# A two-layer streaming encoder on one core: the mixer's element-wise work moved to VectorE, its chains re-spaced, PSUM as one pool of eight banks, and the second half's column sums issued later

## The chip, the core and the metric

The kernel runs on one core of a Trainium2 chip. The engines are PE (TensorE: matrix products, and transposes through the identity), VectorE (DVE), ScalarE (ACT), GpSimd (POOL) and SyncE (SP, which issues the DMAs). PE writes into PSUM, which has eight banks of 512 fp32 columns; VectorE and ScalarE read the banks. The metric is the device time of one execution in microseconds, as the median of several runs.

## What is computed

Two groups of requests share all weights: 512 rows of a new stream and 64 rows of a running one, 576 rows in all, of width 1024. In each of two layers:

```
x = x + 0.5 * post1(SwiGLU_1(pre1(x)))                  # FFN 1, inner width 2816
z = pre2(x) @ w_in                                      # one projection, 2240 columns
mix = concat[MLA(512) | HGRN2(256) | chunk-gMLP(256)] @ w_out
x = x + post2(mix)
x = x + 0.5 * post3(SwiGLU_2(pre3(x)))                  # FFN 2
```

pre and post are RMS norms. The three mixers are:

```
MLA:    c = rmsnorm(kv_a); k_pe = rope(kpe)             # latent, also an output
        p = softmax(q_lat c^T + q_pe k_pe^T), by chunks of 64
        o = (p c) w_uv                                  # 4 heads
HGRN2:  b = cumsum(log f) in a chunk of 64
        S' = exp(b_last) S + sum_s k exp(b_last - b_s) v_s^T
        o  = (q exp(b)) S + (q k^T with decay exp(b_t - b_s), causal) v
        o  = rmsnorm(o, out_g) * silu(g)                # 4 heads of 64
gMLP:   v = rmsnorm(gelu(cv)) ; out = gelu(cu) * (tril(w_s) v + b_s)
```

## The kernel before

Activations stand transposed, the 1024 channels as eight tiles of 128 partitions, the 576 rows as columns, in two **halves** of 288. Each fp32 product is made of three matmuls on a high and a low part (wh and wl of a weight, hh and hl of an activation: L126/L127 split the weights, `split` at L138 to L142 the activations). FFN units (tile u) and projections (tile n) are such triples.

A stage starts with the norm of its input, half by half. `pre` (L185) splits a tile and adds its squares into acc; `pre_stats` then waits, asks PE for the column sums of acc (tile ss, at `colsum`), makes 1/rms (m at L209, the power on GpSimd at L151, tile rn) and, 3.11 us of virtual time later, has PE spread it over the partitions (tile bc). An FFN's units need only hh and hl, and their evacuation needs rbc, the copy of bc. Where the next stage's units are issued among the end of this one, the code calls it packed: mixer to FFN 2 and FFN 2 to layer 1.

In the mixer, five tiles of rows go through w_in. HGRN2's sum over a chunk is cut into seven **levels** h (with two key tiles m each, 14 in all, generator `make(n)` at L700 ff.): two subtractions make differences of b (L707, L708, tile e), ScalarE takes their exponential (L709), GpSimd multiplies by k (L711, tile w), VectorE by q (L717, tile zb, two operations of 64 partitions), PE forms the products lv and ls, and VectorE copies them under a mask into at and ats (L732, L739). Gelu and Silu of the projections (L888, L892) are activations of the tables other than Exp; a change of function between two activations costs a table load. Then state products (su, L819/L821), output norms (`out`, L845/L847, `group_norm` with its power on GpSimd at L151), the gMLP (`cmlp`, L862/L863), latents (`latent`, cn at L908, flipped by PE into cth and ctl), the cache chain (`caches`, ck, kp, cch, ccl), the rotary key, the queries and the attention.

What sets the order: the program is written by one main line that issues the dense products, and a list of background generators. `mul` and `flip` add each product's estimated time to a clock self.t; `tick` resumes a generator once its due time has come, and a `yield 8.0` is a wait of 8 us of that virtual clock. Every engine then runs its instructions in the order in which they were written, except for moves by the scheduler, which keeps that order as a priority; `pin` (keep_in_program_order) forbids such a move. Tiles come from pools: a new tile takes the buffer of an older one and waits until that one's last reader is done. PSUM has the pool mm (six banks) for products and sm (two) for flips, sums and spreads.

## Time and profile before

| | before |
|---|---|
| median of 3 runs | 2283.32 us (2280.43 to 2283.41) |
| profiled execution: its time, its span | 2281.2 us, 2279.4 us |
| mean granted clock of PE | 0.985 |
| PE busy | 2209.0 us, 97% |
| VectorE, ScalarE, GpSimd busy | 1552.8, 1093.7, 157.1 us |

The profile is one execution. Busy time is shown by engine, and the granted clock is a share of 2.4 GHz, with 1.2 GHz as the lower level, so that a window's mean between 0.5 and 1 tells how much of it ran at either. Matmuls are pipelined: one lasts longer than the distance to the next start. "Idle before" an instruction is put down to what released it last. FFN 1 of layer 0 ends at about 440 us, mixer 0 runs from there to about 740, and FFN 2 follows. The transitions named in the prediction are mixer to FFN 2 (at 741 and 1862 us) and FFN 2 to layer 1 (1145 us).

### The profile page before, as it was taken

The numbers are of one execution on the slowest core, as the hardware profiler recorded it, in microseconds if no ns is written. First come the engines' busy times: TensorE is split into PE (matmuls) and PEld (weight loads), VectorE is DVE, ScalarE is ACT, GpSimd is POOL, SyncE is SP. The second block draws the span as 40 slices with busy tenths as digits, with TensorE's granted clock in tenths as the row PEclk, the third lists the DMA queues.
The fourth block names the chain that finished last, engine by engine and source line by source line (L and its number), as shares of the span: only waits on it lengthen the run. The fifth ranks groups of instructions, "written<-read, shape, count | busy, mean of one in ns | idle before, by whom it ended". The sixth has DMA issues, their size and how long they took to land.

```text
span 2279.4 us, 39545 instructions
## 1 busy us (share of the span) xinstructions
PE 2209.0 (97%) x15988; PEld 2152.9 (94%) x15988; DVE 1552.8 (68%) x2697; ACT 1093.7 (48%) x1917; POOL 157.1 (7%) x160
## 2 busy tenths in 40 slices
PE   8999999998899899999999999999988999999998
PEld 8999999988799899999989999998887999999998
DVE  5888643787566888844488875438976578887443
ACT  7454442465554544443354444325746545444423
POOL 0000000143300000000000000001432000000000
PEclk9999999999999999999999999999999999999999
DMA  7333442312212233344223334423121222333421
GB/s 218 91 96 93 121 134 84 105 46 78 62 53 83 90 91 102 87 127 130 61 80 102 93 94 126 128 75 102 40 88 48 75 98 79 94 93 102 121 70 42
DMA packets 339531, 211.07 MB, mean 93 GB/s; under 512 B 17378, under 2 KB 319700, under 8 KB 339348
## 3 DMA queue, kind: packets, MB, share of 16 engines
q1 hardware_dynamic: 339348, 208.54, 30.6%
q8 instruction: 126, 2.06, 0.4%
q14 instruction: 57, 0.47, 0.1%
HBM read 190.11 MB, written 18.38 MB: 91 GB/s over the span
## 4 chain that ended last, share of the span: by engine, by line
PE 83%; DVE 9%; ACT 3%; issue 2%; POOL 2%; DMA 0%; SPq 0%; POOLq 0%; DVEq 0%; ACTq 0%
PE d L68 25%; PE X L68 20%; PE Q L68 10%; PE u L68 9%; PE R L68 5%; PE wo L68 5%; PE n L68 2%; DVE zb L717 1%; PE sc L68 1%; DVE wl L127 1%; PE q L68 1%; DVE hl L142 1%; PE oT L68 1%; POOL gr L151 1%; DVE acc L198 1%
## 5 line engine op out<-in xcount | busy, mean ns | idle before, releaser
L68 PE MATMUL d<-gh,wh 128*128 128x288 f32 x1408 | 414.0, 297 | 2.7 <-ACT gh L138 2.7
L68 PE MATMUL d<-gl,wh 128*128 128x288 f32 x1408 | 414.6, 295 | 0.0
L68 PE MATMUL d<-gh,wl 128*128 128x288 f32 x1408 | 413.5, 295 | 0.0
L127 DVE TENSOR_TENSOR wl<-wr,wh 128x1024 fp32r<-128x1024 f32 (+3 forms) x190 | 222.4, 1176 | 168.4 <-ACT wh L126 167.3
L126 ACT ACTIVATE wh<-wr 128x1024 fp32r<-128x1024 f32 (+3 forms) x190 | 191.6, 1012 | 276.8 <-PE d L68 167.4
L68 PEld LDWEIGHTS d<-gh,wh 128*128 128x128 f32 x1408 | 262.7, 188 | 3.6 <-ACT gh L138 3.6
L68 PEld LDWEIGHTS d<-gh,wl 128*128 128x128 f32 x1408 | 265.2, 189 | 0.0
L68 PEld LDWEIGHTS d<-gl,wh 128*128 128x128 f32 x1408 | 264.3, 188 | 0.0
L68 PE MATMUL X<-th,wh 128*128 128x288 f32 x864 | 256.1, 296 | 0.0
L68 PE MATMUL X<-tl,wh 128*128 128x288 f32 x864 | 255.4, 296 | 0.0
L68 PE MATMUL X<-th,wl 128*128 128x288 f32 x864 | 254.5, 295 | 0.0
L68 PE MATMUL u<-hl,wh 128*128 128x288 f32 x736 | 221.2, 302 | 2.2 <-DVE hl L142 2.0
L68 PE MATMUL u<-hh,wh 128*128 128x288 f32 x736 | 217.3, 305 | 3.0 <-ACT x L1377 1.5
L68 PE MATMUL u<-hh,wl 128*128 128x288 f32 x736 | 219.6, 301 | 0.0
L138 ACT ACTIVATE wh<-wr 128x1024 fp32r<-128x1024 f32 x144 | 151.6, 1056 | 136.1 <-PE R L68 68.5
L139 DVE TENSOR_TENSOR wl<-ws,wh 128x1024 fp32r<-128x1024 f32 x108 | 132.3, 1225 | 102.1 <-ACT wh L138 102.1
L138 ACT ACTIVATE wh<-ws 128x1024 fp32r<-128x1024 f32 x108 | 114.6, 1061 | 148.1 <-DVE ws L508 100.1
L139 DVE TENSOR_TENSOR wl<-wr,wh 128x1024 fp32r<-128x1024 f32 x144 | 175.3, 1220 | 7.4 <-ACT wh L138 6.2
L398 DVE TENSOR_TENSOR d<-d,d 128x288 f32<-128x288 f32 x128 | 55.3, 454 | 181.9 <-PE d L68 181.7
L68 PEld LDWEIGHTS X<-th,wl 128*128 128x128 f32 x864 | 163.1, 189 | 0.0
L68 PEld LDWEIGHTS X<-tl,wh 128*128 128x128 f32 x864 | 162.3, 188 | 0.0
L68 PEld LDWEIGHTS X<-th,wh 128*128 128x128 f32 x864 | 162.1, 188 | 0.0
(364 smaller groups left out, 5562.5 us busy)
## 6 DMA issues: line engine op xcount, KB each, us to landing
wr<-ffn_w_gate SPq DMA_DIRECT2D x144, 256.0 KB, 3.0
wr<-ffn_w_up SPq DMA_DIRECT2D x144, 256.0 KB, 3.4
wr<-ffn_w_down SPq DMA_DIRECT2D x64, 512.0 KB, 4.3
wr<-w_in SPq DMA_DIRECT2D x30, 512.0 KB, 3.7
xd<-x SPq DMA_DIRECT2D x48, 288.0 KB, 2.1
x<-xd SPq DMA_DIRECT2D x48, 288.0 KB, 5.8
wr<-ffn_w_down SPq DMA_DIRECT2D x32, 384.0 KB, 3.6
wr<-ffn_w_gate SPq DMA_DIRECT2D x16, 512.0 KB, 3.7
```

Source lines behind the costliest of these rows:

```text
L68: self.nc.tensor.matmul(out, lhsT, rhs, start=start, stop=stop, skip_group_check=onto)
L126: nc.scalar.activation(hi[:, :a * b], raw[:, :a * b], AF.Copy)
L127: nc.vector.tensor_tensor(lo[:, :a * b], raw[:, :a * b], hi[:, :a * b].bitcast(F32), op=ALU.subtract)
L138: nc.scalar.activation(hi, src, AF.Copy)
L139: nc.vector.tensor_tensor(lo, src, hi.bitcast(F32), op=ALU.subtract)
L142: nc.vector.scalar_tensor_tensor(lo, src, scale, hi.bitcast(F32), op0=ALU.mult, op1=ALU.subtract)
L151: self.nc.gpsimd.tensor_tensor(out, m, self.mhalf[:, :n], op=ALU.pow)
L198: nc.vector.tensor_tensor(self.acc[:, sl], self.acc[:, sl], sq[:, sl], op=ALU.add)
L398: nc.vector.tensor_tensor(d[m][:, sl], d[m][:, sl], ps[hf][:, :n], op=ALU.add)
L717: nc.vector.tensor_tensor(zo, qv[rs, :, h:], ev[rs, :, h:], op=ALU.mult)
```

## The change

- `sm` becomes `mm`: one PSUM pool of eight banks in place of six and two.
- `pre_stats` of the second half waits 14.0 in place of 5.0 where stages are packed, 7.0 elsewhere.
- HGRN2: q times k (L692), the level product and e times k go from GpSimd to VectorE. The level product covers only the first half of each block and is made in place in e. Exp, Gelu and Silu are pinned. The pace of the levels is 2.2 for 3.0.
- Group norm and gate (`out`, `cmlp`) are one operation for each group of 64 columns; hgrn_out_g becomes a scale in the split of the mixed rows (four rows more in the table `more`).
- Query sums (accq) go from GpSimd to VectorE, the PSUM copies of v (L1172) from ScalarE to VectorE.
- The yields of caches, latents, rotary key, query norm, state loop, outputs and gMLP are longer, and the cache and rotary chains are spawned ahead of the query units.

```diff
@@ -56,7 +56,7 @@
         self.t = 0.0
-        self.pace, self.apace, self.l1, self.l2, self.l3 = 3.0, 2.16, 1.26, 3.94, 2.15
+        self.pace, self.apace, self.l1, self.l2, self.l3 = 2.2, 2.16, 1.26, 3.94, 2.15
@@ -109,10 +109,10 @@
     def mm(self, s="mm"):
-        return self.ps.tile([P, 512], F32, name=self.name(s), tag="mm", bufs=6)
+        return self.ps.tile([P, 512], F32, name=self.name(s), tag="mm", bufs=8)
     def sm(self, s="sm"):
-        return self.ps.tile([P, 512], F32, name=self.name(s), tag="sm", bufs=2)
+        return self.mm(s)
@@ -260,7 +260,7 @@
                 yield (1.25, 1.3)[half]
-        yield from self.pre_stats(half, (3.97, 5.0)[half])
+        yield from self.pre_stats(half, 3.97 if half == 0 else 14.0 if self.packed else 7.0)
@@ -569,7 +569,7 @@
             nc.sync.dma_start(kpv[:, :, e], i["cache_mla_kpe"][l, 0].rearrange("(t p) d -> p t d", p=P))
-        yield 8.0
+        yield 14.0
@@ -637,15 +637,15 @@
         self.rsqrt(r, ss, 4)
-        return r.unsqueeze(2).to_broadcast([P, 4, 64])
-
-    def to_mix(self, src, k0, i):
+        return r
+
+    def to_mix(self, src, k0, i, scale=(None, None)):
         for e in range(2):
-            self.split(self.mixh[k0 + e][:, c:c + w], self.mixl[k0 + e][:, c:c + w], ps[:, e * P:e * P + w])
+            self.split(self.mixh[k0 + e][:, c:c + w], self.mixl[k0 + e][:, c:c + w], ps[:, e * P:e * P + w], scale=scale[e])
@@ -692,7 +692,7 @@
             qk.append(self.slot("qk"))
-            nc.gpsimd.tensor_tensor(qk[m], q[m], kk[m], op=ALU.mult)
+            nc.vector.tensor_tensor(qk[m], q[m], kk[m], op=ALU.mult)
@@ -706,16 +706,16 @@
             nc.vector.tensor_tensor(ev[:, :, h:], bv[:, :, h:], rb, op=ALU.subtract)
-            nc.scalar.activation(e[:, c0:], e[:, c0:], AF.Exp)
-            w = self.slot("w")
-            nc.gpsimd.tensor_tensor(w[:, c0:], kk[m][:, c0:], e[:, c0:], op=ALU.mult)
+            self.pin(nc.scalar.activation(e[:, c0:], e[:, c0:], AF.Exp))
                 nc.vector.tensor_tensor(zo, qv[rs, :, h:], ev[rs, :, h:], op=ALU.mult)
-            ready[n] = (w, z)
+            kv = kk[m][:, c0:].rearrange("p (b x) -> p b x", x=2 * h)
+            nc.vector.tensor_tensor(ev[:, :, :h], ev[:, :, :h], kv[:, :, :h], op=ALU.mult)
+            ready[n] = (e, z)
@@ -782,10 +782,10 @@
                                     bv[:, :, P - 1:P].to_broadcast([P, 4, P]), bv, op=ALU.subtract)
-            nc.scalar.activation(e, e, AF.Exp)
+            self.pin(nc.scalar.activation(e, e, AF.Exp))
             eb[m] = self.slot("eb")
-            nc.scalar.activation(eb[m], b[m], AF.Exp)
-            nc.gpsimd.tensor_tensor(e, e, kk[m], op=ALU.mult)
+            self.pin(nc.scalar.activation(eb[m], b[m], AF.Exp))
+            nc.vector.tensor_tensor(e, e, kk[m], op=ALU.mult)
@@ -822,7 +822,7 @@
                         nc.sync.dma_start(dst, new[s, s])
-                yield 0.1
+                yield 1.2
@@ -842,28 +842,29 @@
             on = self.slot("on")
-            nc.vector.tensor_tensor(on[:, :256].rearrange("p (g d) -> p g d", g=4),
-                                    ps[:, :256].rearrange("p (g d) -> p g d", g=4), r, op=ALU.mult)
-            nc.vector.tensor_tensor(on[:, :256], on[:, :256], vg[i][:, 256:512], op=ALU.mult)
-            yield 7.71
-            self.to_mix(on, 4, i)
+            for g in range(4):
+                gs = slice(g * 64, (g + 1) * 64)
+                nc.vector.scalar_tensor_tensor(on[:, gs], ps[:, gs], r[:, g:g + 1], vg[i][:, 256 + g * 64:320 + g * 64],
+                                               op0=ALU.mult, op1=ALU.mult)
+            yield 9.0
+            self.to_mix(on, 4, i, [self.og[:, 2 * l + e:2 * l + e + 1] for e in range(2)])
             self.spawn(out(i))
-            yield 1.12
+            yield 3.2
         r = self.group_norm(v)
-        vv = v.rearrange("p (g d) -> p g d", g=4)
-        nc.vector.tensor_tensor(vv, vv, r, op=ALU.mult)
-        nc.gpsimd.tensor_tensor(v, v, c["vg"], op=ALU.mult)
+        for g in range(4):
+            gs = slice(g * 64, (g + 1) * 64)
+            nc.vector.scalar_tensor_tensor(v[:, gs], v[:, gs], r[:, g:g + 1], c["vg"][:, gs], op0=ALU.mult, op1=ALU.mult)
             nc.sync.dma_start(self.o["cmlp_v"][l, 0], v[:64])
-        yield 4.28
+        yield 8.0
@@ -875,7 +876,7 @@
                                            op0=ALU.add, op1=ALU.mult)
-        yield 6.56
+        yield 8.0
@@ -885,12 +886,11 @@
         for i in range(5):
-            nc.scalar.activation(uv[i][:, :512], uv[i][:, :512], AF.Gelu_apprx_tanh)
-            self.spawn(self.cmlp(l, i, uv[i], c), 0.8 + 2.59 * i)
+            self.pin(nc.scalar.activation(uv[i][:, :512], uv[i][:, :512], AF.Gelu_apprx_tanh))
+            self.spawn(self.cmlp(l, i, uv[i], c), 1.5 + 5.0 * i)
             g = vg[i][:, 256:512]
-            nc.scalar.activation(g, g, AF.Silu)
-            nc.gpsimd.tensor_tensor(g, g, c["og"], op=ALU.mult)
+            self.pin(nc.scalar.activation(g, g, AF.Silu))
@@ -910,7 +910,7 @@
             nc.sync.dma_start(self.o["ckv_p"][l, 0, (i - 1) * P:i * P], cn[:, :256])
-        yield 4.0
+        yield 8.0
@@ -942,7 +942,7 @@
         kpt = a["kpt"] = self.slot("kpth", F32R), self.slot("kptl", F32R)
-        yield 4.0
+        yield 10.0
@@ -950,12 +950,12 @@
                 self.split(kpt[0][:, cs], kpt[1][:, cs], tp[:, e * P:e * P + twid(i)])
-            yield 0.32
+            yield 2.0
         a["sq"] = self.small("sqs", 6, 2)
-        yield 1.34
+        yield 5.0
@@ -1065,7 +1065,6 @@
-        c["og"] = self.gain_rows("hgrn_out_g", l)
@@ -1099,6 +1098,8 @@
             self.step(self.bg[-1])
+        lat.append(self.spawn(self.rotary_key(l, kr, a), 9.0))
+        cg = self.spawn(self.caches(l, c), 0.0)
@@ -1114,9 +1115,7 @@
                     nc.scalar.activation(sq[:, sl], p[:, :n], AF.Square)
-                    nc.gpsimd.tensor_tensor(accq[:, sl], accq[:, sl], sq[:, sl], op=ALU.add)
-        cg = self.spawn(self.caches(l, c), 0.0)
-        lat.append(self.spawn(self.rotary_key(l, kr, a), 1.0))
+                    nc.vector.tensor_tensor(accq[:, sl], accq[:, sl], sq[:, sl], op=ALU.add)
@@ -1169,7 +1168,7 @@
                 self.mul(ps, xl, uw[0][:, ct], False, ct == 1)
-            nc.scalar.activation(t[:, :512], ps, AF.Copy)
+            nc.vector.tensor_copy(t[:, :512], ps)
@@ -1294,8 +1293,8 @@
         ps = self.sm("tp")
-        self.flip(ps[:, :18], more)
-        nc.vector.tensor_copy(self.colg[:, 96:], ps[:, :18])
+        self.flip(ps[:, :22], more)
+        nc.vector.tensor_copy(self.colg[:, 96:], ps[:, :22])
@@ -1326,7 +1325,7 @@
-        pin = tc.keep_in_program_order
+        pin = self.pin = tc.keep_in_program_order
@@ -1353,7 +1352,7 @@
             self.mul(self.warm[:, :P], self.ones, self.ones, True, True)
-        self.colg = const.tile([P, 114], F32, name="colg", tag="colg")
+        self.colg = const.tile([P, 118], F32, name="colg", tag="colg")
@@ -1384,11 +1383,13 @@
         self.ahead += [self.cols(*q) for q in todo[2:4]]
-        more = const.tile([18, P], F32, name="more", tag="more")
+        more = const.tile([22, P], F32, name="more", tag="more")
         nc.sync.dma_start(more[10:18], i["cmlp_b_s"].rearrange("l g t -> (l g) t"))
+        nc.sync.dma_start(more[18:22], i["hgrn_out_g"].rearrange("l (k p) -> (l k) p", p=P))
         self.bs = self.colg[:, 106:114]
+        self.og = self.colg[:, 114:118]
         self.spawn(self.pre_stats(1, 7.5, sums))
```

The first place is PE at the entry of FFN 2 in layer 0. bc is the spread of the first half, ss the column sums of the second, u_8281 and u_8282 are units of the first half, u_8361 and on those of the second. Before:

```order
L68 MATMUL u_8282<-hl_8137,wh_8088 128x288
L68 MATMUL u_8282<-hh_8136,wl_8089 128x288
L73 MATMUL bc_8309<-ident_c,rn_7922 128x64
L73 MATMUL bc_8309<-ident_c,rn_7922 128x128 x2
L68 MATMUL ss_8401<-ones,acc_7920 128x1 x3
L68 MATMUL u_8361<-hh_8164,wh_7796 128x288
L68 MATMUL u_8361<-hl_8165,wh_7796 128x288
L68 MATMUL u_8361<-hh_8164,wl_7797 128x288
```

After:

```order
L68 MATMUL u_8461<-hh_8164,wl_8083 128x288
L68 MATMUL u_8462<-hh_8164,wh_8088 128x288
L68 MATMUL u_8462<-hl_8165,wh_8088 128x288
L68 MATMUL u_8462<-hh_8164,wl_8089 128x288
L68 MATMUL ss_8475<-ones,acc_7920 128x1 x3
L68 MATMUL u_8461<-hh_8207,wh_8082 128x288
L68 MATMUL u_8461<-hl_8208,wh_8082 128x288
L68 MATMUL u_8461<-hh_8207,wl_8083 128x288
```

ss now stands 108 rows behind the first u_8361 (u_8461 and u_8462 are the last of these 108), where it stood just ahead of it.

The second place is PE at the entry of mixer 0: ss are the column sums of the first half and bc its spread, u_4818 and u_4819 before (u_4819 and u_4820 after) units whose half follows. Before:

```order
L68 MATMUL u_4611<-hh_4688,wl_4358 128x288
L68 MATMUL ss_4764<-ones,acc_4454 128x1 x3
L68 MATMUL u_4612<-hl_4689,wh_4363 128x288
L68 MATMUL u_4612<-hh_4688,wl_4364 128x288
L68 MATMUL u_4818<-hh_4502,wl_4346 128x288
...
L68 MATMUL u_4818<-hh_4594,wh_4345 128x288
L73 MATMUL bc_4809<-ident_c,rn_4456 128x64
L73 MATMUL bc_4809<-ident_c,rn_4456 128x128 x2
```

After:

```order
L68 MATMUL u_4613<-hl_4690,wh_4364 128x288
L68 MATMUL ss_4765<-ones,acc_4455 128x1 x3
L68 MATMUL u_4613<-hh_4689,wl_4365 128x288
L73 MATMUL bc_4810<-ident_c,rn_4457 128x64
L73 MATMUL bc_4810<-ident_c,rn_4457 128x128 x2
L68 MATMUL u_4819<-hh_4503,wh_4346 128x288
L68 MATMUL u_4819<-hl_4504,wh_4346 128x288
```

Between ss and bc stood 25 matmuls, and one is left; the others follow bc.

The third place is VectorE among the levels, where e_5189 (before) and e_5208 (after) are the differences of one level. Before:

```order
L127 TENSOR_TENSOR wl_5555<-wr_5552,wh_5554 128x960
L732 COPY_PREDICATED at_5090<-lmask_c,lv_5212 128x8x32
L732 COPY_PREDICATED at_5092<-lmask_c,lv_5212 128x8x32
L739 COPY_PREDICATED ats_5063<-lmask_c,ls_5219 64x2x32
L717 TENSOR_TENSOR zb_5007<-z_4608,e_5189 64x288 x2
L707 TENSOR_TENSOR e_5222<-b_5025 128x18x16
L708 TENSOR_TENSOR e_5222<-b_5025 128x18x16
L127 TENSOR_TENSOR wl_5561<-wr_5558,wh_5560 128x960
```

After:

```order
L732 COPY_PREDICATED at_5090<-lmask_c,lv_5198 128x8x32
L739 COPY_PREDICATED ats_5061<-lmask_c,ls_5205 64x2x32
L708 TENSOR_TENSOR e_5208<-b_5024 128x18x16
L127 TENSOR_TENSOR wl_5249<-wr_5246,wh_5248 128x1024
L715 TENSOR_TENSOR zb_5008<-z_4608,e_5208 64x288 x2
L717 TENSOR_TENSOR e_5208<-e_5208,k_5012 128x18x16
L732 COPY_PREDICATED at_5119<-lmask_c,lv_5258 128x8x32
L732 COPY_PREDICATED at_5121<-lmask_c,lv_5258 128x8x32
L739 COPY_PREDICATED ats_5061<-lmask_c,ls_5265 64x2x32
```

The multiplication of e by k, which was GpSimd's, stands behind the zb pair; the lines moved by two (zb is L715 now, the new product L717).

## Rows read from the trace of the kernel before

**Rows 1.** The page, part 1: busy time of each engine, share of the span, instructions.
```profile
PE 2209.0 (97%) x15988; PEld 2152.9 (94%) x15988; DVE 1552.8 (68%) x2697; ACT 1093.7 (48%) x1917; POOL 157.1 (7%) x160
```

**Rows 2.** Windows: each engine's busy us (instructions), granted PE clock, DMA share, GB/s.
```profile
520.00:540.00 20.00, 16.14 (x99) 15.19 (x98) 17.00 (x33) 11.89 (x20) 5.76 (x5) 0.84 0.33 103
600.00:620.00 20.00, 15.86 (x80) 13.40 (x80) 8.79 (x28) 13.84 (x33) 3.21 (x3) 0.83 0.11 30
620.00:640.00 20.00, 18.12 (x123) 17.36 (x122) 12.06 (x29) 11.31 (x27) 0.98 (x1) 0.91 0.09 27
627.00:684.00 57.00, 57.00 (x430) 55.05 (x429) 34.21 (x103) 31.62 (x83) 0.00 (x0) 0.98 0.19 54
741.00:764.00 23.00, 17.06 (x111) 16.51 (x110) 20.90 (x49) 13.97 (x31) 2.72 (x2) 0.85 0.35 126
1145.00:1170.00 25.00, 19.53 (x133) 18.98 (x132) 22.55 (x56) 13.77 (x33) 2.68 (x3) 0.86 0.35 123
1862.00:1890.00 28.00, 22.05 (x147) 21.51 (x147) 25.04 (x59) 15.38 (x34) 3.71 (x3) 0.82 0.35 123
```

**Rows 3.** Timeline of PE in mixer 0: start us, duration us, operation, tiles.
```profile
531.49 0.31 PE L68 MATMUL n<-wh,hl 128*128 128x320 f32 x1
...
536.41 0.47 PE L68 MATMUL n<-wl,hh 128*128 128x320 f32 x1
```

**Rows 4.** Waits of PE from 440 to 660 us: total us, times, longest us.
```profile
PE tp L73 <- DVE cn L908: 3.9, 1, 3.9
PE v L68 <- ACT cch L138: 2.2, 1, 2.2
...
PE lv L68 <- DVE zb L717: 1.0, 1, 1.0
...
PE tp L73 <- ACT kd L803: 0.3, 1, 0.3
```

**Rows 5.** Waits of PE over the whole span.
```profile
PE ss L68 <- DVE acc L198: 16.3, 3, 5.4
```

**Rows 6.** Timeline of PE at the entry of FFN 2, layer 0; [idle before it and its releaser].
```profile
756.94 1.44 PE L68 MATMUL ss<-ones,acc 128*128 128x1 f32 x6 [5.42 <-DVE acc L198]
```

**Rows 7.** Timeline of PE and VectorE at the entry of mixer 0.
```profile
431.45 0.72 PE L68 MATMUL ss<-ones,acc 128*128 128x1 f32 x6
...
435.41 0.16 DVE L209 TENSOR_SCALAR m<-ss 128x3 f32<-128x3 f32 x1
...
436.55 0.63 PE L73 MATMUL bc<-ident_c,rn 64*128 64x64 f32 x3 [0.44 <-POOL rn L151]
```

**Rows 8.** Timeline of VectorE in the levels of mixer 0.
```profile
500.01 0.77 DVE L732 COPY_PREDICATED at<-lmask_c,lv 128x256 f32<-128x256 int32 x2
...
500.81 0.44 DVE L707 TENSOR_TENSOR e<-b 128x288 f32<-128x288 f32 x1
501.18 0.44 DVE L708 TENSOR_TENSOR e<-b 128x288 f32<-128x288 f32 x1
502.37 2.07 DVE L717 TENSOR_TENSOR zb<-z,e 64x288 f32<-64x288 f32 x2 [0.75 <-ACT e L709]
```

**Rows 9.** Timeline of GpSimd beside the last of these.
```profile
502.42 1.71 POOL L711 TENSOR_TENSOR w<-k,e 128x576 f32<-128x576 f32 x1 [2.75 <-PE ls L68]
```

**Rows 10.** Line 717 over the span: ns min/median/max, first and last start.
```profile
L717 DVE TENSOR_TENSOR zb<-z,e x56: 416/480/1687, 467.9 to 1658.0; 64x288 f32<-64x288 f32 x48, 64x256 f32<-64x256 f32 x8
```

**Rows 11.** Groups of PE from 440 to 540 us: busy us, mean ns | idle before.
```profile
L68 PE MATMUL lv<-zb,w 128*128 128x128 f32 x104 | 13.8, 276 | 1.0 <-DVE zb L717 1.0
```

**Rows 12.** Timeline of ScalarE in the levels.
```profile
504.23 0.63 ACT L888 ACTIVATE uv<-uv 128x512 f32<-128x512 f32 x1
504.88 1.28 ACT L709 ACT_TABLE_LOAD   x1
506.17 0.68 ACT L709 ACTIVATE e<-e 128x576 f32<-128x576 f32 x1
```

**Rows 13.** Groups of VectorE from 440 to 640 us.
```profile
L139 DVE TENSOR_TENSOR ccl<-tp,cch 128x512 fp32r<-128x512 f32 x1 | 0.7, 691 | 2.6 <-ACT cch L138 2.6
```

## The prediction

> **What bounds the kernel now.** The engine row of the page comes first: PE is busy 97% of the span, VectorE 68%, ScalarE 48%, GpSimd 7% [rows 1]. A change can only gain where PE idles or where its clock is down, so I next read PE's windows. A dense stretch from 627 us has 430 matmuls in 57 us at clock 0.98; in mixer 0 the windows at 520, 600 and 620 us have PE busy 16 to 18 of 20 us and clocks of 0.84, 0.83 and 0.91, and each of the three entries into an FFN that shares its work with the stage ahead (741, 1145 and 1862 us) shows about 0.85 [rows 2]. The clock falls behind an idle stretch: a matmul of PE took 0.31 us at 531.49, then PE stood 3.9 us for cn, and the same form then took 0.47 [rows 3, 4].
>
> What PE waits for, from 440 to 660 us: 14 waits, from 3.9 us on a late latent row (cn) down to 0.3 [rows 4], 16.2 us in all. They are single late steps of chains, not one slow engine. Outside the mixers one wait stands out, the column sums ss that wait for acc: three times, 16.3 us [rows 5].
>
> So one mixer loses 16.2 us of waits plus the clock. Time lost to the clock is (1 - clock) times the window: (0.16 + 0.17 + 0.09) x 20 = 8.4 us [rows 2]. **24.6 us per mixer, two mixers** (in the second the same waits stand again). The three transitions lose 16.3 us of waits and 0.15x23 + 0.14x25 + 0.18x28 = 12.0 us of clock, **28.3 us**.
>
> **The change part by part.**
>
> Column sums asked for later. At 751.5 us PE finds ss next in its queue and stands 5.42 us for the last acc [rows 6], with ready matmuls of the second half behind it. The new order has 108 of them ahead of ss. At 0.133 us (57 us / 430) these are 14.4 us, so ss finds acc done. What is late next: behind ss the rn chain has 30 matmuls, 4.0 us, before bc is wanted. At 435 us that chain took 1.1 us (m at 435.41, bc at 436.55) [rows 7]; a VectorE backlog of 2 us is covered too. Two smaller waits are new: the post-factor's broadcast stands 10 matmuls behind its column sum where it stood 22, 1.3 us for a chain of 1.1 us plus its place in VectorE's queue; I take a stall of 1.4, bounds 0 and 2, and 0.7 for the next broadcast, bounds 0 and 1.5. Should one of the three transitions still drop the clock, 3.4 us come back (the drop at 533 us gave 0.16 x 20 = 3.2). 28.3 - 3x2.1 - 3.4 = **18.6 us gained**, bounds 10 and 28.
>
> Products on VectorE (qk, the level products, e times k). The level product becomes one more 288-column operation per level on VectorE. Such an operation lasts 0.44 us and the next starts 0.37 later; three copies of a level take 0.80 from start to start [rows 8]. The other side is the zb products: two took 2.07 us at 502.37, with a GpSimd product of 1.71 us running from 502.42 [rows 8, 9], but the smallest of 56 is 0.416 and the median 0.48 [rows 10]. I take 0.37 from start to start once GpSimd is quiet. A level is then five times 0.37 plus 0.80, 2.65 us; fourteen are 37. With six weight splits of 1.2 and some 3.5 of other work VectorE has 48 us. PE's order from the first level to the last has 153 projection matmuls (150 before, and 63 shorter ones that now come later), 36 us at 0.236 each (0.133 by 512/288 columns), and level products of 13.8 us busy [rows 11] with the small ls beside them, about 51 us with ls at 0.2 us for each of 11 and the overlaps off: 36 + 13.8 + 2.2 - 1. VectorE just keeps up, so I price this at nothing for PE; the bound on the other side, zb at 1.03, is rival B.
>
> Pinned activations. ScalarE loads a table 26 times less; 26 x 1.28 = 33 us [rows 12], and PE gets none of it directly. The price: five Gelu, five Silu and two loads stand in one block ahead of the copy that a state product su needs. With Gelu at 0.63 on the row and Silu, half as wide, below it, the block is at most 8.9 us; following the order with these durations su waits 1.3 us, about what it waits now, bounds 0 and 4. One load is followed at once: it starts at 504.88, lasts 1.28, and the next activation starts at 506.17 [rows 12].
> The Trainium skill ("ScalarE: Activation LUTs", section "What ACT_TABLE_LOAD costs") gives a drain of about 1.38 us beside the 1.28 of a load. The rows show no such drain; by the page the block's two loads would hold su 2.8 us longer per mixer, and the time would be 5.5 us above the forecast.
>
> Group norm and gate in four steps of 64 columns: two more instructions on each of 20 chains, below 0.37 us each, so under 0.8 us on a chain, which now has 3.2 or 5 us of spacing and PE's other work over it: nothing. The dropped gain multiplies were on GpSimd, nothing either.
>
> Later yields, earlier caches. The waits for cn (3.9), cch (2.2) and the smaller ones of caches, latents and rotary key go: their transposes stand 4 to 6 us deeper in PE's order, or the chain is spawned some 9 us earlier. Left, by the order and these durations: lv 1.1 at the first two levels (now 1.0), su 1.3, about 1.0 of small ones. A new one is in the tail: the v copies go from ScalarE to VectorE, 0.69 each by the same shape [rows 13], into a queue of 25 instructions with the rotary chain, and the bank that a q needs is held by one of them. Bounds 0 and 5 (seven copies); I take 2.9, since 22 us of matmuls stand against 16 us of VectorE work plus its waits for ScalarE. Together 6.3 us; one such wait drops the clock briefly, 1.7 us, as the 0.09 x 20 of the window at 620.
>
> One pool of eight banks. It also moves the entry of each mixer: today 25 matmuls stand between ss and bc, now one. ss starts at 431.45 and ends by 432.2; bc can start at 436.55 [rows 7], so PE stands 4.4 us. The 25 matmuls (3.3 us) now run behind bc, where PE today waits in pieces of 0.2 to 0.5 us for hl. Net between 1.0 and 2.9, I take 1.7. An idle of 4.4 us is like the 3.9 and 5.4 that dropped the clock: 3.4 us more, bounds 0 and 3.4.
>
> **Sum.** A mixer keeps 6.3 + 1.7 + 1.7 + 3.4 = 13.1 of its 24.6 us, a gain of 11.5; two are 23.0. With 18.6 from the transitions 41.6. From the profiled 2281.2 us that gives 2239.6; the median of the runs stands 2.1 above that execution, so **2241 us** with rounding. All terms good (no drop at the entry, 2x3.4; transitions 9 better; tail 0, 2x2.9): 2220. All bad (tail 2x2.1, entry 2x1.2, transitions 8, su 2x2.7): 2261.
>
> **The rivals.**
>
> A: only the transitions gain. The waits of a mixer sit on spread chains, and each that is removed exposes the next, which the trace can't show since it was never last; a mixer gives 2 us, not 11.5. For it: 14 waits, not one. Against it: the new order puts microseconds of ready matmuls ahead of most of them. 2283.3 - 18.6 - 4 = 2261.
>
> B: VectorE becomes the bound of the levels. If zb needs 1.03 us whatever GpSimd does, a level is 2.65 + 2x0.66 = 3.97 and VectorE has 66 us against PE's 51: 15 us per mixer, 2241 + 30 = 2271. Against it: half of the zb rows at 0.48 or less [rows 10].
>
> C, the slower side: B's wait comes as about 1.1 us at each of 14 levels, and PE's clock is down over the whole stretch, as it was after waits of that size in the window at 600 [rows 2]. PE's 51 us of work would need 102 at half clock in place of the 66: 36 more at most; a third of it, 12 us per mixer, makes 2271 + 24 = 2295. It decides from where a mixer loses 21 us more than forecast: 15 of waits and 6 of clock, 12 us at the lower level.
>
> D: the change doesn't do what it says: ss is out of the way, but the second half's units wait for banks which the first half's evacuation still holds. Then the transitions give 5 and the mixers their 23: 2255.
>
> **How the numbers follow.** Chances: the forecast (2230 to 2252) 0.56; better 0.10; A or D (2253 to 2264) 0.18; B 0.07; within 0.2% of 2283.3 (4.6 us, about what a measurement here can tell) 0.03; C or another loss 0.06. So faster 0.91, same 0.03, slower 0.06. From 2220 to 2264 lie the forecast, most of the better case, A and D: 0.83.
>
> **What would show it.** Right: no wait of ss behind acc; a clock of 0.98 or more over the three transitions; a pitch between levels of 51/13 = 3.9 us; zb at 0.45; no cn or cch wait; at each mixer's entry a wait of 4 us for rn. Wrong: zb still at 1 us; waits of lv for zb at most levels; q or k waiting over 5 us for a bank; a transition whose wait has moved to bc or to a bank of u.

## The result, and the profile after

The changed kernel takes **2252.23 us** (median of 4 runs, 2250.07 to 2254.23) beside 2282.52 for the kernel before: ratio 0.9868, 95% interval 0.9855 to 0.9881, so 30 us or 1.3% faster. The forecast was 2241 in a range of 2220 to 2264: the direction and the range held, and 11 us of the 42 forecast did not come.

The engine row of the page after, to be read beside [rows 1]:

```profile
PE 2194.2 (98%) x15988; PEld 2140.4 (95%) x15988; DVE 1540.6 (69%) x2805; ACT 1054.0 (47%) x1877; POOL 69.5 (3%) x96
```

PE runs the same 15,988 matmuls. GpSimd lost more than half of its time, ScalarE 40 us (26 table loads and 14 v copies), and VectorE is no busier with 108 more instructions.

**The transitions.** The windows over the three entries into an FFN, as long as the last three of [rows 2] and begun 7 to 9 us earlier in the program, so that the new waits ahead of the old one fall into them (columns as there):

```profile
725.00:748.00 23.00, 21.25 (x158) 20.32 (x157) 21.55 (x53) 11.17 (x27) 1.84 (x2) 1.00 0.32 114
1125.00:1150.00 25.00, 22.99 (x174) 22.53 (x174) 23.64 (x57) 11.84 (x29) 1.83 (x2) 1.00 0.33 117
1830.00:1858.00 28.00, 26.22 (x196) 25.29 (x195) 26.55 (x65) 14.94 (x34) 1.85 (x2) 1.00 0.30 107
```

The clock is 1.00 in all three, and spans of the same length hold 158, 174 and 196 matmuls where they held 111, 133 and 147. 47 + 41 + 49 = 137 more, at 0.133 us each 18.2 us. That is the gain of the transitions; taken from one matmul ahead of each entry to one behind it, the same two in both traces, it is 18.3.

**The mixers.** From the first projection matmul to the first of w_out mixer 0 took 203.1 us before and takes 194.8 now, mixer 1 202.0 and 192.9: 17.4 us less in sum. These four stretches, the first two before and the others after (span less PE's busy time is its idle time):

```profile
449.13:652.22 203.09, 187.03 (x1151) 166.60 (x1150) 149.56 (x346) 118.77 (x231) 64.54 (x54) 0.96 0.23 66
1575.72:1777.74 202.02, 185.46 (x1152) 164.84 (x1150) 152.20 (x350) 118.78 (x231) 61.87 (x54) 0.97 0.21 65
...
450.71:645.53 194.82, 182.39 (x1152) 162.15 (x1151) 146.69 (x402) 100.00 (x213) 19.72 (x22) 0.99 0.23 68
1560.23:1753.11 192.88, 182.59 (x1152) 162.14 (x1150) 148.86 (x406) 100.03 (x213) 21.16 (x22) 0.99 0.23 67
```

Their entries cost more than before: in the 22 us ahead of the first projection of mixer 0 PE had 149 matmuls and has 123, ahead of mixer 1 148 and 123, so 26 + 25 matmuls or 6.8 us. 18.2 + 17.4 - 6.8 = 28.8 us, against 31.1 between the two profiled spans; the rest came in before the first mixer, whose first projection starts only 1.6 us later than before although its entry lost 3.5. These last two us are no more than noise: e6, e7 and e10 below differ from the changed kernel only behind that point and reach it 1.6 to 2.8 us later than it does. PE's waits from 440 to 660 us, beside [rows 4] (us in total, times, longest):

```profile
PE q L68 <- DVE v L1171: 3.8, 3, 2.7
PE su L68 <- DVE cn L908: 2.1, 1, 2.1
PE su L68 <- ACT kdn L799: 2.0, 1, 2.0
PE tp L73 <- DVE on L847: 1.2, 1, 1.2
PE lv L68 <- DVE e L717: 1.0, 2, 0.8
PE v L68 <- DVE on L847: 0.6, 1, 0.6
PE u L68 <- DVE on L847: 0.6, 1, 0.6
PE pt L73 <- DVE rv L1003: 0.5, 1, 0.5
PE dq L68 <- DVE qk L695: 0.4, 1, 0.4
PE o L68 <- DVE on L847: 0.3, 1, 0.3
```

12.5 us in thirteen waits, where there were 16.2 in fifteen (ten and fourteen lines of the view). The waits for the late latent row's flip, for cch, ck and kd are gone. In their place stand waits of a product for a row that it doesn't read: su for cn, v and u for on, q for a v copy. By the code, such a product waits for its PSUM bank, whose last tile the named instruction reads.

At the mixer's entry, beside [rows 7], the spread of the first half as PE's timeline shows it:

```profile
434.81 0.98 PE L73 MATMUL bc<-ident_c,rn 64*128 64x64 f32 x3 [4.15 <-POOL rn L151]
```

and the windows of 22 us that end with each mixer's first projection, the first two before, the others after, with the lower clock behind the wait (the last is the window at 620 us of [rows 2]):

```profile
427.10:449.10 22.00, 20.44 (x149) 19.24 (x148) 20.13 (x48) 10.09 (x22) 4.87 (x11) 1.00 0.51 172
1553.70:1575.70 22.00, 20.41 (x148) 19.20 (x147) 20.05 (x47) 10.10 (x22) 4.86 (x11) 1.00 0.52 177
...
428.70:450.70 22.00, 17.85 (x123) 17.52 (x123) 14.77 (x37) 7.17 (x16) 3.96 (x11) 0.84 0.42 151
1538.20:1560.20 22.00, 17.79 (x123) 17.32 (x122) 14.92 (x38) 7.33 (x17) 3.95 (x11) 0.92 0.43 153
...
620.00:640.00 20.00, 19.54 (x139) 18.71 (x138) 13.12 (x42) 12.63 (x32) 0.00 (x0) 0.92 0.07 21
```

The zb products (line 715 now), beside [rows 10] (ns minimum/median/maximum):

```profile
L715 DVE TENSOR_TENSOR zb<-z,e x56: 417/450/458, 472.9 to 1627.6; 64x288 f32<-64x288 f32 x48, 64x256 f32<-64x256 f32 x8
```

No zb takes more than 0.46 us where the slowest took 1.69.

### The profile page after: what moved, and what is told of

It reads as the page before. It is cut to its first block, busy times and chain, and to the rows that moved or that the text cites. A ratio compares the mean times of both kernels' runs of the same rounds, so it can differ in the third digit from the quotient of the medians.

```text
span 2248.3 us, 39455 instructions
## 1 busy us (share of the span) xinstructions
PE 2194.2 (98%) x15988; PEld 2140.4 (95%) x15988; DVE 1540.6 (69%) x2805; ACT 1054.0 (47%) x1877; POOL 69.5 (3%) x96
## 4 chain that ended last, share of the span: by engine, by line
PE 87%; DVE 7%; ACT 3%; POOL 2%; issue 2%; DMA 0%; SPq 0%; POOLq 0%; DVEq 0%; ACTq 0%
PE d L68 25%; PE X L68 20%; PE Q L68 10%; PE u L68 9%; PE R L68 5%; PE n L68 5%; PE wo L68 4%; PE sc L68 1%; PE lv L68 1%; POOL gr L151 1%; PE oT L68 1%; PE q L68 1%; DVE hl L142 1%; DVE wl L127 1%; PE k L68 1%
```

## The experiments

Each time is a median; the ratio is to the kernel before on the same chip. A difference to the changed kernel is taken from its 2252.2 us, which was measured in another set of runs, so that one or two microseconds of it say nothing.

| run | what it is | us | ratio, 95% interval |
|---|---|---|---|
| | before | 2282.5 | |
| | changed kernel | 2252.2 | 0.9868 [0.9855, 0.9881] |
| e1 | before, late column sums alone | 2285.3 | 1.0015 [1.0006, 1.0025] |
| e2 | changed, early column sums | 2252.7 | 0.9877 [0.9862, 0.9892] |
| e3 | before, one pool alone | 2272.3 | 0.9961 [0.9946, 0.9976] |
| e4 | changed, two pools | 2289.8 | 1.0034 [1.0022, 1.0047] |
| e5 | changed, products on GpSimd | 2273.1 | 0.9959 [0.9944, 0.9974] |
| e6 | changed, v copies on ScalarE | 2254.6 | 0.9881 [0.9866, 0.9896] |
| e7 | changed, no pins | 2250.3 | 0.9863 [0.9847, 0.9880] |
| e8 | changed, sum and spread share a bank | 2247.8 | 0.9848 [0.9833, 0.9862] |
| e9 | before, products on VectorE alone | 2274.2 | 0.9969 [0.9958, 0.9980] |
| e10 | changed, last v copies ahead | 2252.1 | 0.9869 [0.9856, 0.9883] |
| e11 | e8 + e10 + Gelu and Silu spread | 2244.1 | 0.9837 [0.9823, 0.9850] |
| e12 | before, one pool and products | 2259.6 | 0.9901 [0.9884, 0.9917] |

### What freed the transitions: the later request or the pool

e1, on the kernel before:

```diff
-        yield from self.pre_stats(half, (3.97, 5.0)[half])
+        yield from self.pre_stats(half, 3.97 if half == 0 else 14.0 if self.packed else 7.0)
```

> The kernel before with one edit: the second half's column sums are asked for 14.0 (packed) or 7.0 us later, as in the changed kernel; two PSUM pools stay. Theory of the prediction (the later request is what takes ss out of PE's way): the three waits of ss for acc go, 15 to 18 us faster, about 2266. Rival (the pool of eight banks is what lets the second half's units go ahead of ss): with two pools PE's order still has ss right behind bc of the first half, so the three waits of 5.4 us stay and the time is 2280 to 2285.

e2 is the same line undone in the changed kernel.

> The changed kernel with one edit undone: the second half's column sums are asked for after 5.0 us everywhere, as before; one pool of eight banks stays. Theory of the prediction: the three waits come back, 15 us slower, about 2267. Rival (the pool does it): ss stands some 66 units, 8.8 us, behind bc instead of 124, 16.5 us, which is still longer than the wait of 5.4, so the time stays within 4 us of 2252.

e3, on the kernel before:

```diff
-        return self.ps.tile([P, 512], F32, name=self.name(s), tag="mm", bufs=6)
+        return self.ps.tile([P, 512], F32, name=self.name(s), tag="mm", bufs=8)
...
-        return self.ps.tile([P, 512], F32, name=self.name(s), tag="sm", bufs=2)
+        return self.mm(s)
```

> The kernel before with one edit: one pool of eight PSUM banks. If the pool is what frees the transitions: the three waits of ss for acc go (15 us), each mixer's entry gets the wait of 4.2 us for rn and a lower clock for some 7 us (about +1.6 net per mixer as measured between the two kernels), and the mixers change by what bank waits cost or give. About 2268 if the mixers are neutral; 2280 or more if waits for banks in the mixers cost 6 us each. If the later request does it: the waits stay, about 2283 to 2290.

e4 is that edit undone in the changed kernel.

> The changed kernel with the two PSUM pools of before (six banks and two). If the pool frees the transitions: the three waits of ss for acc are back, +15 us; the wait for rn at each mixer's entry goes, -3 us; in the mixers the waits of su behind cn, of u, o and v behind on and of q behind v copies (7.8 us in mixer 0) are bank waits and go or change place. 2255 to 2265. If the later request freed them: 2240 to 2250, below the changed kernel.

The later request alone gave nothing (3 us slower). In e1's waits of PE over the span the row of [rows 5] stands unchanged:

```profile
PE ss L68 <- DVE acc L198: 16.3, 3, 5.4
```

Nor does the early request hurt in the changed kernel (2252.7). One pool alone does at the transition what the changed kernel does; e3's window there, to be read beside the 158 matmuls above:

```profile
734.00:757.00 23.00, 21.24 (x158) 20.31 (x157) 21.55 (x54) 10.90 (x27) 1.85 (x2) 1.00 0.32 113
```

In the kernel before 144 matmuls, six units of the first half, stand ahead of the spread bc at this entry: they hold the six banks. As the order reads, the second half's units had to wait for one of these, and ss came ahead of them however late it was written (in e1 it still follows bc at once). With eight banks in one pool more were there for units, and these went ahead: in e3 66 matmuls of units stand between bc and ss. Over the three transitions e3 gains the same 18.3 us as the changed kernel. So the step was priced right and put down to the wrong edit.

e3 pays for it elsewhere: at the mixers' entries, and with longer waits for late rows of the chains in their old spacing. Of its waits over the span:

```profile
PE tp L73 <- DVE cn L908: 11.9, 4, 4.5
PE bc L73 <- POOL rn L151: 8.4, 2, 4.2
PE v L68 <- ACT cch L138: 7.1, 2, 4.1
```

cn was 7.9, cch 4.8 and rn 2.9 before. The flips read cn itself, so that these are not waits for a bank: in mixer 0 the first cn is done 87.1 us behind the first projection, where it was 86.5, and PE now comes to the last flip 1.5 us ahead of its cn. From the first projection to w_out its mixers take 202.4 and 204.7 us, no less than the 203.1 and 202.0 of before. And e4 shows the other side: without the pool the rest of the change is a loss, 7 us against the kernel before and 37.5 against the changed one. The ss wait of 16.3 us is back, as the row of e4 says:

```profile
PE ss L68 <- DVE acc L198: 16.3, 3, 5.4
```

and its mixers take 207.9 and 202.6 us with the clock down in longer stretches; two windows of mixer 0 in e4:

```profile
580.00:600.00 20.00, 14.91 (x73) 13.17 (x72) 11.46 (x46) 6.11 (x18) 3.79 (x4) 0.62 0.23 66
620.00:640.00 20.00, 15.53 (x88) 13.32 (x87) 13.89 (x27) 12.96 (x28) 1.43 (x1) 0.91 0.09 27
```

### What the products on VectorE gave

e5, on the changed kernel: qk, the level product (whole blocks, into a tile w) and e times k back on GpSimd.

```diff
-            nc.vector.tensor_tensor(qk[m], q[m], kk[m], op=ALU.mult)
+            nc.gpsimd.tensor_tensor(qk[m], q[m], kk[m], op=ALU.mult)
...
+            w = self.slot("w")
+            nc.gpsimd.tensor_tensor(w[:, c0:], kk[m][:, c0:], e[:, c0:], op=ALU.mult)
...
-            kv = kk[m][:, c0:].rearrange("p (b x) -> p b x", x=2 * h)
-            nc.vector.tensor_tensor(ev[:, :, :h], ev[:, :, :h], kv[:, :, :h], op=ALU.mult)
-            ready[n] = (e, z)
+            ready[n] = (w, z)
...
-            nc.vector.tensor_tensor(e, e, kk[m], op=ALU.mult)
+            nc.gpsimd.tensor_tensor(e, e, kk[m], op=ALU.mult)
```

> The changed kernel with the three products (q times k, the level product, e times k) back on GpSimd, all else changed. Theory of the prediction (GpSimd beside VectorE makes the zb products slow): zb rises from 0.45 to about 1 us, a level costs VectorE 2 x 0.58 - 0.37 = 0.8 us more, 11 us per mixer, and PE waits for zb where VectorE had kept up: the stretch from the first to the last level grows from 53.4 to 58 us or more, 2262 or more. Rival (the stretch got shorter only because 63 projection matmuls left it): zb may slow, but the stretch stays within 1.5 us and the time within 4 us of 2252.

20.9 us slower, in the main by the mechanism expected; part of it is the flip's wait for the GpSimd product e itself, 5.2 us in both mixers. In e5 zb (line 717 there) is at 1.0 us again, in the groups of VectorE from 440 to 640 us and, below, in PE's waits over the span:

```profile
L717 DVE TENSOR_TENSOR zb<-z,e 64x288 f32<-64x288 f32 x24 | 24.1, 1003 | 5.7 <-ACT e L709 5.5
```

```profile
PE lv L68 <- DVE zb L717: 9.5, 10, 2.5
...
PE tp L73 <- POOL e L788: 5.2, 2, 2.6
```

The stretch from the first to the last level grows from 53.4 to 59.1 us, the next one, up to the first state product, from 14.2 to 18.3. This is rival B with its cause present: the VectorE bound of the levels is real, and what keeps the changed kernel from it is that GpSimd is quiet.

e9 is the same edit alone, on the kernel before.

> The kernel before with one edit: the three products (q times k, the level product on half of each block, e times k) on VectorE. Theory: zb falls from 0.96 to 0.45 us and VectorE gains some 9 us per mixer, but PE was never waiting there (20.00 us busy of 20 in the windows at 480 and 500 us, one wait of lv of 1.0 us), so the stretch of the levels changes only by the late cn behind it (3.9 us and its clock drop of 3.4, both in that stretch): 0 to 7 us per mixer, 2268 to 2282. Rival (the products gain by themselves what the undo of them cost in the changed kernel, 20.8 us): 2262.

8.3 us faster, in the middle of the 2268 to 2282 expected. e9's zb is at 0.45:

```profile
L715 DVE TENSOR_TENSOR zb<-z,e x56: 411/450/483, 474.1 to 1652.1; 64x288 f32<-64x288 f32 x48, 64x256 f32<-64x256 f32 x8
```

The stretch of the levels fell from 69.2 to 60.2 us, since cn now comes in time: VectorE starts the first one 82.4 us behind the first projection, where it was 86.0, and no flip waits for it. So the product edit has a gain of its own that the prediction put down to later yields.

e12 joins it with one pool.

> The kernel before with two edits: one pool of eight PSUM banks and the three products on VectorE; yields, pins, group norm, v copies and the order of caches as before. Alone these two gave 9.6 and 8.3 us. If they only add: 2264.5, and the 12 us to the changed kernel are what the later yields, the earlier caches and the pins give. If they explain the whole change: 2252. If the yields matter in a pool of eight banks in particular: the waits for cn and cch, 19 us in all with one pool alone, are still there in size (over 12 us) at 2262 or more.

2259.6, 23.4 us below the 2282.9 of the kernel before in the same set of runs: three quarters of the whole, and 5 us more than the 17.9 that the two would add up to, a surplus within the intervals of the three runs. The waits for cn shrink from e3's 11.9 to 1.4 us; cch stays:

```profile
PE bc L73 <- POOL rn L151: 8.4, 2, 4.2
PE v L68 <- ACT cch L138: 7.0, 2, 4.1
...
PE tp L73 <- DVE cn L908: 1.4, 2, 0.8
```

The third possibility of the expectation fell with that. What is left for the yields, the earlier caches and the other edits together is 7 us; the earlier cache chain has the cch wait of 7.0 to take away. The pins (e7), the v copies (e6) and the late sums (e2) change nothing alone; the yields, the caches and the group norm weren't run one by one.

### The late steps that are left in the mixer

e6, on the changed kernel:

```diff
-            nc.vector.tensor_copy(t[:, :512], ps)
+            nc.scalar.activation(t[:, :512], ps, AF.Copy)
```

> The changed kernel with the v copies back on ScalarE. If their place in VectorE's queue is what holds the banks: the waits of q for v copies (5.4 us in both mixers, 3.8 of it in the first) and the two short clock drops of 3.4 us at half behind them go, 6 to 9 us faster, 2243 to 2246. If any evacuation there is late (before, with ScalarE, k and q waited 3.7 us for the same copies): a gain of 0 to 3 us, 2249 to 2252.

No gain (2254.6, above both of the ranges expected). PE waits for the same copy on the other engine, 5.2 us for 5.4:

```profile
PE q L68 <- ACT v L1171: 5.2, 3, 2.4
```

So it isn't the engine. The copy that q waits for is that of the last two v tiles, which the program writes behind the second rotary query: its eight swaps (ScalarE, 3.31 us), a GpSimd product of 1.44 and VectorE's part. e10 writes these two ahead:

```diff
-        rope(5)
         self.finish([cg])
         for j in range(5, 7):
             value(j)
+        rope(5)
```

> The changed kernel with the last two value products and their copies written ahead of the second rotary query instead of behind it. Theory: the copy that frees the bank which q wants stands in order behind that rotary chain (ScalarE 3.3 us, GpSimd 1.4, VectorE), on whichever engine; written ahead of it, the longest wait of q (2.7 and 1.6 us) and the short clock drop behind it (1.7) go in both mixers: 5 to 8 us faster, 2244 to 2247. Rival (the bank just passes the wait on to the rotary query, which now comes later, and heads two and three wait): 2250 to 2254.

The wait of q for v is gone, and the time is the same (2252.1). The rival held; the wait went on to the scores, of which e10's row over the span tells:

```profile
PE sc L68 <- ACT kth L138: 5.1, 2, 3.3
```

The tail of the mixer is a chain through ScalarE, GpSimd and VectorE that is as late as before by whatever product meets it first.

e7 takes the pins away, five edits of this form in the changed kernel:

```diff
-            self.pin(nc.scalar.activation(e[:, c0:], e[:, c0:], AF.Exp))
+            nc.scalar.activation(e[:, c0:], e[:, c0:], AF.Exp)
```

> The changed kernel without the pinned order of Exp, Gelu and Silu. Theory: the block of ten activations and two loads is what makes su wait for the key copy (3.9 us in both mixers); without pins these waits go and table loads come back (26 x 1.28 = 33 us of ScalarE, which is busy 47%): 2 to 4 us faster, 2248 to 2250. Rival: loads between Exp and Silu delay the level chain: lv waits for e and zb come up, 3 us or more slower.

2250.3, the same within the interval. The wait of su for the key copy is gone and PE's waits from 440 to 660 us sum to 7.6 us for 12.5, as the theory had it. The rival's waits of lv did not come up; the product dq, ahead of the levels, waits for qk a little longer than the 0.4 us of the changed kernel, and the clock is down around it. Whether this low clock or the spread between executions took back what the waits gave, one profile doesn't tell. e7's row of that wait, and its window:

```profile
PE dq L68 <- DVE qk L695: 0.8, 1, 0.8
```

```profile
460.00:480.00 20.00, 19.16 (x82) 15.88 (x81) 11.94 (x22) 12.00 (x18) 0.58 (x1) 0.83 0.11 29
```

### The mixer's entry, and the best version

With one pool the second half's first unit takes the bank given out eight tiles earlier: four units of the first half, the sum and the spread of the post norm, the sum and the spread of the pre norm are eight, so it is a first-half unit's bank, which is free only when rn has been spread. e8 uses one bank for a sum and its spread:

```diff
-    def spread(self, r, half, runs=None):
+    def spread(self, r, half, runs=None, ps=None):
...
-        ps = self.sm("bc")
+        ps = self.sm("bc") if ps is None else ps
...
-        bc = self.spread(p, half)
+        bc = self.spread(p, half, ps=bank)
```

(and the same in `pre_stats`; `post_factor` returns its bank too).

> The changed kernel with one PSUM bank for a column sum and the spread that follows it (the spread overwrites the sum, which has been read by then). Theory: at a mixer's entry the second half's first units wait since the eighth bank before is one that a first-half unit holds until rn is spread; with one bank less in the rotation they run between ss and the spread, the wait of 4.2 us for rn and the drop of the clock for 6.8 us go in both mixers: about 3 us per mixer (lost time at the entry 6.6 to 3.5 us), 2246. The transitions stay as they are. Rival (VectorE's chain of the entry is the bound whatever PE does): the first projection starts as late as now, 2252 within 2 us.

2247.8, 4.5 us faster: the wait for rn is back to the 0.44 of before, with the units between (the spread is tile ss here):

```profile
436.48 0.63 PE L73 MATMUL ss<-ident_c,rn 64*128 64x64 f32 x3 [0.44 <-POOL rn L151]
```

The wait is gone, so the mechanism is shown; its worth is less sure, for the interval overlaps that of the changed kernel. At mixer 0's entry 158 matmuls stand in the last 22 us where there were 123, 4.7 us at one entry, while the whole kernel gained 4.5. In the mixers behind it the clock is lower than the changed kernel's 0.99:

```profile
425.90:447.90 22.00, 21.21 (x158) 20.29 (x156) 19.26 (x47) 8.92 (x20) 4.52 (x11) 1.00 0.49 165
447.88:643.33 195.45, 184.68 (x1153) 164.95 (x1150) 146.70 (x402) 99.99 (x213) 20.07 (x23) 0.97 0.24 69
1556.75:1749.60 192.85, 183.75 (x1152) 163.84 (x1150) 148.84 (x406) 99.91 (x213) 21.53 (x23) 0.98 0.24 69
```

e11 adds e10's edit and yields between the pinned Gelus and Silus:

```diff
             self.spawn(self.cmlp(l, i, uv[i], c), 1.5 + 5.0 * i)
+            yield 0.8
...
             self.pin(nc.scalar.activation(g, g, AF.Silu))
+            yield 0.6
```

> The changed kernel with the shared bank for sum and spread, the last value copies ahead of the second rotary query, and Gelu and Silu spread by yields of 0.8 and 0.6 us, still pinned, so that the second key copy comes after two Gelus instead of ten activations. If the three are independent: -4.5 (measured), -6 (q and clock), -4 (su behind the key copy): about 2238. If PE meets the next late row each time: 2243 to 2247.

2244.1 (2242.8 to 2247.6), 38 us below the kernel before, and its interval ends below that of the changed kernel. It is the second case: of the 8.1 us below the changed kernel 4.5 are e8's, the other two edits add 3.6, where e8's and e11's intervals still overlap, and the waits that went (su, q) left time to the next ones (sc for kth, u and v for on).

## Why the prediction was right, and where it was off

- **The bound and the places.** PE's idle time and its clock, in the mixers and at three transitions: right. All of the gain that is clear of noise lies there. The 2252.2 us stand at the outer edge of what the prediction called the forecast (2230 to 2252), next to A or D.
- **Transitions, 18.6 us.** Measured 18.2. The mechanism named (the later request) was wrong: the pool of eight banks does it (e1 to e4). The order had been read for the changed kernel as a whole, where ss stands 108 matmuls later; an order with that one line alone would have told the edits apart. The new stalls were 1.75 us of PE idle in the first window against 2.1 forecast. One error hid in the working: the clock's loss was counted over the whole window, idle time with it. Part of the low clock falls into PE's wait, where it costs nothing, as a window of the kernel before inside the cn wait shows (below). The deduction for a clock drop that did not come (3.4) covered it in part. Waits were to give 16.3 - 6.3 = 10.0 us and the clock 12.0 - 3.4 = 8.6; by the windows PE's idle time fell by 11.8, which leaves 6.4 for the clock. That the sum agrees to half a us is luck.
- **Products on VectorE, nothing for PE.** Right on zb (0.45) and on VectorE keeping up; wrong at "nothing". Undone they cost 20.9 us (e5) and alone they give 8.3 (e9): cn stands in the same VectorE queue and came 3.6 us sooner, a gain that the prediction had put down to the later yields.
- **Pinned activations.** su waits for the key copy 2.0 us; forecast 1.3, bounds 0 to 4. The sentence on the table-load drain stays without support: in the changed kernel, as in [rows 12], the next activation starts 0.01 us behind most loads, and undoing the pins with 24 more loads left the time as it was.
- **Later yields.** cn, cch, ck and kd did go, partly by the products (e12).
- **The tail, 2.9 us, one short clock drop.** Measured: one wait of 2.7 us, 3.8 in all, and a clock of 0.92 in the window of 20 us at 620, 1.6 us. The cause given, VectorE's queue, was wrong (e6, e10).
- **The entry.** The wait was 4.15 us (forecast 4.4), the clock over the 22 us 0.84 in mixer 0, as forecast, and 0.92 in mixer 1; 26 and 25 matmuls fewer are 3.4 us per entry where 1.7 + 3.4 = 5.1 stood.
- **The terms that were mis-sized are "Left ... together 6.3 us" and the clock of the mixers.** PE's idle time is 12.4 us in mixer 0 and 10.3 in mixer 1, 10 us more than twice 6.3. Missing in mixer 0 were bank waits of the one pool ahead of the tail, su for cn 2.1 and u, v and o for on 1.5, and the flip's wait for on itself, 1.2. The prediction weighed the pool at the entry alone. (Its 14 waits are lines of the view; they are 15 waits.) The clock was to give 8.4 - 1.7 = 6.7 us per mixer, 13.4 in all. The two mixers became 17.4 us shorter and PE's idle time in them 9.9, which leaves 7.5 for the clock: 6 us less. One reason is that mixer 1, taken to be like mixer 0, had a clock of 0.97 over its 202 us, a loss of about 6 and not 8.4. The rest fits a part of the low clock that fell into PE's idle time and had been counted twice; it wasn't measured by itself. 10 + 6, less the 3.4 by which the entries cost less than put down and the 2 of the start, make the 11 us between forecast and result. The window of the kernel before, inside the wait for cn:

```profile
534.00:535.50 1.50, 0.00 (x0) 0.00 (x0) 0.65 (x4) 0.00 (x0) 0.56 (x1) 0.50 0.56 160
```

  PE ran nothing there and the clock is at the lower level all the same.
- **Rivals.** A (the next late step takes over) holds for the last waits, as those of e10 and e11 show; as the forecast of the whole it was 9 us off. B needs GpSimd's products, as e5 shows. C did not come: e4's mixers came nearest, by another way. D was wrong for the transitions, though banks were in fact the point of that place.

## What to carry to other kernels

Read a PSUM pool as part of the order: which tile's bank a product takes decides where it may stand, so that a split into pools can hold matmuls behind a sum that nothing but the split puts ahead of them. A wait of a product for an instruction whose result it doesn't read is a wait for a buffer: cure it by fewer tiles in the rotation (e8) and not by moving the reader to another engine (e6). When several edits come together, look at each one's order by itself before a gain is put down to it: here one that looked decisive gave nothing, and two others gave three quarters of it.

## What the runs showed of the hardware

- A VectorE product of two SBUF tiles (64 x 288, fp32) takes 0.45 us alone. In the kernel before 28 of the 56 take 0.50 to 1.69 us, 1.47 on average, and each of these 28 overlaps GpSimd's product of k and e; the mean of all is 0.96. In e5 the slowest takes 1.73. All 56 are at 0.46 or below once GpSimd is left with small operations only.
- The clock's answer to idle time can't be read from one idle stretch. In the changed kernel two waits of 1.95 and 2.07 us for su, 12 us apart, left the clock at 1.00; in e8 nearly the same pair (1.96 and 2.06) was followed by the lower clock, 0.91 in the window. The changed kernel's window, then e8's:

```profile
540.00:560.00 20.00, 15.98 (x121) 15.26 (x119) 10.83 (x44) 12.90 (x35) 3.96 (x6) 1.00 0.28 91
```

```profile
550.00:570.00 20.00, 17.94 (x123) 16.61 (x123) 15.99 (x69) 6.82 (x21) 4.28 (x6) 0.91 0.34 102
```

- A table load takes 1.28 us on ScalarE, and 24 more of them (e7) left the time as it was. It doesn't come with each change of function: the changed kernel has 17 loads among 1877 instructions of ScalarE, with Copy and Square between the others.
